# Attention's first and last probabilities scaled half by ScalarE and half by VectorE, with low parts, maxima and score products reordered

## The chip, the core and the metric

The kernel runs on one core of one Trainium2 chip. The metric is the device time of one execution in microseconds (us). Before the change three runs gave 2219.98, 2221.18 and 2222.38 us; the median is 2221.18.

The engines are named as in the profile: PE is TensorE (PEld its weight loads), DVE is VectorE, ACT is ScalarE, POOL is GpSimd, SP is the queue that issues the transfers.

## The reference

One layer of a hybrid decoder runs over 2048 prompt tokens and 64 sample tokens. The part that the change touches is sliding-window attention with 8 query heads, 2 key heads, head size 64 and a window of 128; each block of 128 queries sees its own and the previous block of keys:

```
scores = jnp.where(mask, scores, -jnp.inf)
m = jnp.maximum(jnp.max(scores, axis=-1, keepdims=True), sink)
p = jnp.exp(scores - m)
return p / (jnp.sum(p, axis=-1, keepdims=True) + jnp.exp(sink - m))
...
out = jnp.einsum('bnhgqk,bnkhd->bnqhgd', p.astype(v.dtype), vv)
```

Beside it stand the input projection, gated linear attention, the output projection and the MLP, which the change leaves as they are.

## The kernel before

**Number format.** Products are wanted at about fp32 accuracy, so nearly every operand exists twice: a rounded high part, made by ACT with a copy, and a low part, made by DVE as the source minus the high part. A product is then two or three matmuls.

**Stages.** The first stage, some 310 us, projects the tokens and does the attention; gated linear attention, the output projection and the MLP follow. The loop of this stage (lines 782 and after) runs over 16 blocks of 128 tokens, i = 0 to 15. Each iteration does the attention of block i in four **units** and in between, as filling for PE, the projection of block i + 2, the transposes of block i + 3 and the heads of block i + 1. A unit is one pair of heads: unit (i, r, jj) is key head r, pair jj; in an iteration u = 0 to 3 stand for (0,0), (0,1), (1,0), (1,1). The names in the order rows carry them: `s_11_1_0` is the score tile of block 11, r = 1, jj = 0.

**A unit's steps** (lines 457 to 527), each ended by a `yield`:

1. `sc`: four score matmuls on PE.
2. two maxima on DVE, one for each head of the pair, which also write the masked scores to `s` (the custom operation CUSTOM_DVE_ANT_0, ISA in the order rows); each gives a column of `m`.
3. two exponentials on ACT, each with its column of `m`, which also give the sums `den`.
4. reciprocal of `den` on DVE, then two multiplications of `s` by it, on DVE; in unit (1,1) both on ACT.
5. `pT`: four transposes on PE (two for each head of the pair).
6. `ph`: high part of `pT`, on ACT. 7. `pl`: low part, on DVE.
8. `av`: four matmuls of `ph` and `pl` with the values. 9. `rest`: a copy on ACT. 10. `mo`: an addition on DVE.

**What sets the order.** PE, ACT and DVE each take their instructions in the order in which the program writes them; `InOrder` (line 110) chains every call made through `te`, `ac` and `dv`. The program writes them by stepping three units through their `yield`s by hand: `now` (maxima to `ph`), `behind` (the unit before, `pl` to `mo`) and `ahead` (the unit after, `sc`). One turn of the loop over u (line 821) is called a **slot** below; slot u has unit u as `now`. POOL and SP are ordered by the scheduler.

**Other work in the slots** is placed by the table `A_PLAN` (line 58): a name, the slot, and a letter for the place within it; T stands after the first step of `now`, A after the exponentials, X after the transposes of `x`, B after `pT`, C after `ph`. What the prediction speaks of: `xT`, the transposes of block i + 3 (`x_half`, line 288), with `xh` (ACT) and `xl` (DVE); `junk`, a sum of squares on ACT in slot 2; `first` and `rest`, which scale a projection into `qk`, `glr` and `vv` on ACT, and `vl`, the low parts of `vv` and `glr` on DVE; and from `heads_T` (line 404), run in slot 2 for block i + 1, the transposes `pq` and `pk`, the high parts `qh`, `kh` and `ql` (ACT; `ql` holds the high part for r = 1 in its upper half), and the low parts `klo0`, `lo0`, `lo1` on DVE. `xT` and `pq` share one PSUM bank, so that `xT` waits until the low parts of the queries have been read from it.

**PE's filling** is `A_FILL` (line 56): so many projection matmuls at three places of each slot, 13, 12, 10 and 13 in slots 0 to 3.

Of the kernel before, what the change touches and what calls it, by code (L numbers as in the profile page):

```python
# [55 lines left out]
A_FILL = ((11, 2, 0), (10, 0, 2), (10, 0, 0), (12, 1, 0))  # L56
A_LEAD, A_SPLIT = 14, (2, 1, 0, 0)
A_PLAN = [(name, (int(at[0]), at[1])) for name, at in dict(
    klo0="3T", first="1B", hi1="3B", x1="1B", lo1="0A", x0="0C", rest="3A", lo0="3A", junk="2A", turn="1A", rstd="1A", vl="3B"
).items()]  # L60
G_FIRST = (0, 1)
G_NEXT = (NB, *range(2, NB))
# [77 lines left out]
def hybrid_step_kernel(ctx: ExitStack, tc: tile.TileContext, I, O):  # L140
# [263 lines left out]
    def heads_T(i):  # L404

        n, rot = rows(i), rots.pop(i)
        if i == NB - 1:
            stores.append((O["k_win_prompt"][0, 0].rearrange("w h d -> w (h d)"), rot[:, 4].rearrange("p r d -> p (r d)")))  # L410
        if i == NB:
            for name, new in (("k", rot[:, 4].rearrange("p r d -> p (r d)")), ("v", vals[i])):
                stores.append((new_d[name], new[:NS]))
        pq = bank([P, 4, P], "d", f"pq_{i}")
        for j in range(4):
            te.transpose(pq[:, j, :n], rot[:n, j].rearrange("p r d -> p (r d)"), ident[:n, :n])
        pk = bank([P, P], "b", f"pk_{i}")
        te.transpose(pk[:, :n], rot[:n, 4].rearrange("p r d -> p (r d)"), ident[:n, :n])
        if i == NB:
            qs = sp.tile([P, DB, 4, DT], F32, tag="tb", name="qs", bufs=1)  # L420
            ac.activation(qs, pq[:, :, :NS].rearrange("p j (b t) -> p b j t", b=DB), AF.Copy, scale=0.125)
            kns = sp.tile([P, NS], F32, name="kns")
            ac.activation(kns, pk[:, :NS], AF.Copy)
            heads[i] = qs, kns
            return {}
        qs = [sp.tile([P, 4, P], F32R, tag=t, name=f"{t}_{i}", bufs=2) for t in ("qh", "ql")]
        ks = sp.tile([P, 2, 2, P], F32R, tag="kh", name=f"kh_{i}", bufs=2)
        kl = sp.tile([P, 2, 2, P], F32R, tag="kl", name=f"kl_{i}", bufs=2)
        ac.activation(qs[0][half_of[0]], pq[half_of[0]], AF.Copy, scale=-0.125)
        for r in range(2):  # L430
            ac.activation(ks[half_of[r], r, 1, :], pk[half_of[r]], AF.Copy)
            if i > 0:
                nc.gpsimd.tensor_copy(ks[half_of[1 - r], r, 1, :], f32(ks[half_of[r], r, 1, :]))
            else:
                ac.activation(ks[half_of[1 - r], r, 1, :], pk[half_of[r]], AF.Copy)
        if i > 0:
            nc.gpsimd.tensor_copy(ks[:, :, 0, :], f32(heads[i - 1][1][:, :, 1, :]))
            nc.gpsimd.tensor_copy(kl[:, :, 0, :], f32(heads[i - 1][2][:, :, 1, :]))
        heads[i] = qs, ks, kl

        def k_lo(r):
            dv.tensor_tensor(kl[half_of[r], r, 1, :], pk[half_of[r]], f32(ks[half_of[r], r, 1, :]), op=ALU.subtract)
            nc.gpsimd.tensor_copy(kl[half_of[1 - r], r, 1, :], f32(kl[half_of[r], r, 1, :]))

        def q_lo(r):
            dv.scalar_tensor_tensor(
                qs[r][half_of[1 - r]], pq[half_of[r]], -0.125, f32(qs[r][half_of[r]]), op0=ALU.mult, op1=ALU.subtract
            )

        return {  # L450
            "klo0": lambda: k_lo(0),
            "lo0": lambda: q_lo(0),
            "hi1": lambda: ac.activation(qs[1][half_of[1]], pq[half_of[1]], AF.Copy, scale=-0.125),
            "lo1": lambda: (k_lo(1), q_lo(1)),
        }

    def unit(i, r, jj, mo):

        nkt = min(i + 1, 2)
        nk = nkt * P  # L460
        rr = half_of[r]
        u_ = f"{i}_{r}_{jj}"
        h0 = r * 4 + jj * 2
        s = sp.tile([P, 2, nk + 1], F32, tag="s", name=f"s_{u_}", bufs=3)
        nc.gpsimd.tensor_copy(s[:, :, nk : nk + 1], sink[:, h0 : h0 + 2].unsqueeze(2))
        yield
        qs, ks, kl = heads[i]
        kh, kl = (t[:, r].rearrange("p a k -> p (a k)")[:, 2 * P - nk :] for t in (ks, kl))
        sc = bank([P, 2, nk], "b", f"sc_{u_}")
        for u in range(2):  # L470
            j = jj * 2 + u
            te.matmul(sc[:, u, :], qs[r][:, j, :], kh, start=True, stop=False)
            te.matmul(sc[:, u, :], qs[r][:, j, :], kl, start=False, stop=True)
        yield
        m = sp.tile([P, 2], F32, tag="m", name=f"m_{u_}", bufs=3)
        for u in range(2):
            dv.tensor_tensor_reduce(
                s[:, u, :nk], sc[:, u, :], amask[:, 2 * P - nk :], scale=1.0,
                scalar=sink[:, h0 + u : h0 + u + 1], op0=ALU.add, op1=ALU.min, accum_out=m[:, u : u + 1],
            )  # L480
        yield
        den = sp.tile([P, 2], F32, tag="den", name=f"den_{u_}", bufs=3)
        for u in range(2):
            ac.activation(
                s[:, u, :], s[:, u, :], AF.Exp, scale=-1.0, bias=m[:, u : u + 1], accum_out=den[:, u : u + 1]
            )
        yield
        dv.reciprocal(den, den)
        for u in range(2):
            if (r, jj) == (1, 1):  # L490
                ac.activation(s[:, u, :nk], s[:, u, :nk], AF.Copy, scale=den[:, u : u + 1])
            else:
                dv.tensor_scalar(s[:, u, :nk], s[:, u, :nk], den[:, u : u + 1], None, op0=ALU.mult)
        yield
        pT = bank([P, nkt, 2, P], "c", f"pT_{u_}")
        for u in range(2):
            for kt in range(nkt):
                te.transpose(pT[:, kt, u, :], s[:, u, kt * P : (kt + 1) * P], ident)
        yield
        ph = sp.tile([P, nkt, 2 * P], F32R, tag="ph", name=f"ph_{u_}", bufs=2)  # L500
        pl = sp.tile([P, nkt, 2 * P], F32R, tag="pl", name=f"pl_{u_}", bufs=2)
        pf = pT.rearrange("p k u q -> p k (u q)")
        ac.activation(ph, pf, AF.Copy)
        yield
        dv.tensor_tensor(pl, pf, f32(ph), op=ALU.subtract)
        yield
        av = bank([P, 2 * P], "e", f"av_{u_}")
        vs = [vals[t] for t in range(i + 1 - nkt, i + 1)]
        both, hi, lo = ([v[:, r, u] for v in vs] for u in (slice(2), 0, 1))
        both = [v.rearrange("p u d -> p (u d)") for v in both]  # L510
        out = mo[rr, jj * 2 : jj * 2 + 2].rearrange("p j q -> p (j q)")
        if nkt == 1:
            te.matmul(av[:HD], hi[0], ph[:, 0], start=True, stop=False)
            te.matmul(av[:HD], hi[0], pl[:, 0], start=False, stop=False)
            te.matmul(av[:HD], lo[0], ph[:, 0], start=False, stop=True)
            yield
            ac.activation(out, av[:HD], AF.Copy)
        else:
            te.matmul(av, both[0], ph[:, 0], start=True, stop=False)
            for kt in range(2):  # L520
                te.matmul(av[:HD], hi[kt], pl[:, kt], start=False, stop=False)
            te.matmul(av, both[1], ph[:, 1], start=False, stop=True)
            yield
            rest = sp.tile([P, 2 * P], F32, tag="spc", name=f"rest_{u_}", bufs=2)
            ac.activation(rest[:HD], av[HD:], AF.Copy)
            yield
            dv.tensor_tensor(out, av[:HD], rest[:HD], op=ALU.add)
        if (r, jj) == (1, 1):
            stores.append((mix_d[i][:, 0:4, :], mo))
        yield  # L530
# [135 lines left out]
    def run(products, n=None):  # L666
        deque(products if n is None else islice(products, n), 0)
# [118 lines left out]
    for i in range(NB):  # L786
# [34 lines left out]
        for u in range(4):  # L821
            next(now)
            do(u, "T")
            next(behind, None)
            next(now)
            do(u, "A")
            later = next(queue)
            next(later)
# [2 lines left out]
            if u != 3:  # L831
                next(behind, None)
            run(fill, A_FILL[u][1])
            if u < 2 and new:
                hi, todo[f"x{u}"] = x_half(i + 3, u)
                hi()
            elif u == 2:
                todo.update(heads_T(i + 1))
            do(u, "X")
            run(fill, A_FILL[u][2])  # L840
            next(now)
            if u == 3:
                next(behind, None)
            next(behind, None)
            next(ahead)
            next(now)
            do(u, "B")
            split_some(A_SPLIT[u] if i < NB - 1 else 1)
            next(now)
            do(u, "C")  # L850
            behind, now, ahead = now, ahead, later
    for left in todo.values():
        left()
# [1263 lines left out]
```

## Time and profile before

| | |
|---|---|
| three runs | 2219.98, 2221.18, 2222.38 us |
| the profiled execution | 2222.0 us, span 2220.2 us |
| busy, whole span | PE 2172.9, DVE 1518.6, ACT 1218.7, POOL 261.7 us |
| busy, 61.58 to 284.64 us (iterations 1 to 13, from slot 2 to slot 2) | 223.06 us: PE 215.96, ACT 186.06, DVE 178.66, POOL 133.90 |

The span is the profiled execution without what lies before its first and after its last instruction. A busy time is the time in which an engine has an instruction running; PE's matmuls overlap and their ends are modelled, so that PE can look busy while it waits, and its waits are better read from the distance of the starts. In a timeline row stand start, duration, engine, line, operation, output and inputs, and in square brackets the idle time ahead of it and what ended it. Nearly all rows name line 129, that of the helper, so tiles tell them apart.

### The profile page before, as it was taken

The page shows a single profiled execution, that of the slowest core. Times are in us where ns is not written, and L with a number is a line of the kernel's source. Part 1 is how long each engine was busy: PE and PEld are TensorE (multiplying, and loading weights), DVE is VectorE, ACT ScalarE, POOL GpSimd, SP SyncE. Part 2 cuts the span into 40 slices and gives each one's busy share as a digit, 9 for nine tenths or more (in the row PEclk, how much of TensorE's full clock was granted, in tenths as well). Part 3 has the DMA queues.
Part 4 walks back from the last instruction along what each step waited for, and adds up shares of the span by engine and source line. Part 5 has one row for each costly group of instructions (what it writes and reads, how often), then busy time and mean ns, then how long its engine had stood idle before and what let it go on. Part 6 is the DMA issues. An engine that isn't in the chain of part 4 may idle for free.

```text
span 2220.2 us, 34144 instructions
## 1 busy us (share of the span) xinstructions
PE 2172.9 (98%) x11784; PEld 1863.6 (84%) x11784; DVE 1518.6 (68%) x3101; ACT 1218.7 (55%) x2626; POOL 261.7 (12%) x417
## 2 busy tenths in 40 slices
PE   8999999999999999899999999999999999999998
PEld 7889888999998888688888887888888888888886
DVE  5888777777876665788888655547776666555566
ACT  6788866556664443555555554435454545444444
POOL 3566522111111100000000000000000000000000
PEclk9999999999999999999999999999999999999999
DMA  7344322214436665867877677767553444666685
GB/s 236 121 137 146 104 90 84 67 58 132 152 110 230 205 194 192 256 218 256 277 272 244 242 238 233 235 192 259 186 186 140 148 157 147 227 199 196 194 267 188
DMA packets 240010, 411.53 MB, mean 185 GB/s; under 512 B 25877, under 2 KB 142077, under 8 KB 235725
## 3 DMA queue, kind: packets, MB, share of 16 engines
q1 hardware_dynamic: 239836, 409.35, 55.7%
q8 instruction: 93, 1.52, 0.3%
q14 instruction: 81, 0.66, 0.1%
HBM read 266.34 MB, written 143.98 MB: 185 GB/s over the span
## 4 chain that ended last, share of the span: by engine, by line
PE 77%; DVE 9%; ACT 8%; DMA 3%; issue 2%; POOL 1%; SPq 0%; DVEq 0%; ACTq 0%; POOLq 0%
PE dn L129 25%; PE gproj L129 9%; PE uc L129 7%; PE ua L129 7%; PE out L1269 6%; PE ud L129 4%; PE ub L129 4%; PE ue L129 4%; ACT s L129 2%; PE proj L129 2%; PE sam L129 1%; PE dsam L129 1%; DVE s L129 1%; PE o L129 1%; PE xT L129 1%
## 5 line engine op out<-in xcount | busy, mean ns | idle before, releaser
L129 PE MATMUL dn<-o0t,o0s 128*128 128x512 f32 x896 | 349.3, 390 | 2.4 <-ACT f L1891 1.1
L129 PE MATMUL dn<-o1t,o0s 128*128 128x512 f32 x896 | 349.5, 390 | 0.5 <-DVE o1t L217 0.5
L129 PE MATMUL dn<-o0t,o1s 128*128 128x512 f32 x896 | 349.3, 390 | 0.0
L217 DVE TENSOR_TENSOR o1s<-rs,o0s 128x512 fp32r<-128x512 f32 x224 | 154.8, 691 | 231.2 <-ACT o0s L216 228.4
L216 ACT ACTIVATE o0s<-rs 128x512 fp32r<-128x512 f32 x224 | 141.1, 631 | 305.8 <-PE dn L129 283.8
L129 PE MATMUL gproj<-wg,gx 128*128 128x384 f32 x1408 | 264.7, 342 | 2.9 <-ACT dec L1025 1.8
L129 PEld LDWEIGHTS gproj<-wg,gx 128*128 128x128 f32 x1408 | 241.0, 188 | 7.8 <-issue 3.9
L129 ACT ACTIVATE st<-st 128x512 f32<-128x512 f32 x224 | 141.2, 630 | 141.9 <-DVE st L129 137.9
L129 PEld LDWEIGHTS dn<-o0t,o0s 128*128 128x128 f32 x896 | 168.2, 188 | 39.9 <-ACT f L1891 1.5
L129 PEld LDWEIGHTS dn<-o1t,o0s 128*128 128x128 f32 x896 | 168.2, 188 | 37.4 <-DVE o1t L217 1.4
L129 PEld LDWEIGHTS dn<-o0t,o1s 128*128 128x128 f32 x896 | 168.2, 188 | 35.2
L129 PE MATMUL uc<-H,s 128*128 128x512 f32 x768 | 187.7, 393 | 1.7 <-ACT s L129 1.2
L129 PE MATMUL ua<-H,w 128*128 128x512 f32 x744 | 179.2, 390 | 0.0
L129 PEld LDWEIGHTS uc<-H,s 128*128 128x128 f32 x768 | 143.6, 189 | 33.2 <-ACT s L129 1.6
L129 PEld LDWEIGHTS ua<-H,w 128*128 128x128 f32 x744 | 139.7, 188 | 29.4
L1269 PE MATMUL out<-wo,mt 128*128 128x512 f32 x680 | 158.6, 392 | 0.0
L217 DVE TENSOR_TENSOR o1t<-rt,o0t 128x512 fp32r<-128x512 f32 x224 | 153.5, 685 | 7.5 <-ACT o0t L216 7.3
L206 POOL TENSOR_TENSOR frs<-rs_v,half 128x1 f32<-128x1 f32 (+1 forms) x13 | 10.1, 787 | 1214.7 <-DVE rs_v L204 693.5
L1269 PEld LDWEIGHTS out<-wo,mt 128*128 128x128 f32 x680 | 126.5, 188 | 26.1
L216 ACT ACTIVATE o0t<-rt 128x512 fp32r<-128x512 f32 x224 | 138.2, 617 | 8.5 <-DMA rt<-t_d 8.2
L129 DVE TENSOR_TENSOR st<-st 128x512 f32<-128x512 f32 x160 | 110.6, 691 | 26.6 <-ACT st L129 22.3
L129 ACT ACTIVATE s<-t 128x1024 fp32r<-128x1024 f32 x62 | 65.7, 1060 | 96.8 <-PE ua L129 27.9
(393 smaller groups left out, 4224.8 us busy)
## 6 DMA issues: line engine op xcount, KB each, us to landing
s_d<-st SPq DMA_DIRECT2D x32, 1792.0 KB, 9.8
rs<-s_d SPq DMA_DIRECT2D x224, 256.0 KB, 2.9
raw<-in_w_up SPq DMA_DIRECT2D x64, 512.0 KB, 4.6
rt<-t_d SPq DMA_DIRECT2D x128, 256.0 KB, 4.4
rt<-in_w_down SPq DMA_DIRECT2D x96, 256.0 KB, 3.2
t<-in_w_down SPq DMA_DIRECT2D x64, 256.0 KB, 4.1
t_d<-t SPq DMA_DIRECT2D x32, 512.0 KB, 3.4
gx<-xt_d SPq DMA_DIRECT2D x28, 512.0 KB, 6.0
```

The costliest lines, as they stand in the source:

```text
L129: ins = call(*a, **k)
L206: nc.gpsimd.tensor_tensor(out, v[:n], e, op=ALU.pow)
L216: nc.scalar.activation(hi, src, AF.Copy)
L217: vector.tensor_tensor(lo, src, f32(hi), op=ALU.subtract)
L1269: te.matmul(banks[c], x, w[:, c * 512 : (c + 1) * 512], start=k + u == 0, stop=k == KT - 1 and u == len(products) - 1,)
```

## The change

It moves five things and splits one:

- The two maxima of a unit are now two steps, and `pl` of the unit before is written between them.
- The probabilities of units (0,0) and (1,1) are scaled half by ACT (the first head) and half by DVE (the second); before, DVE did both of (0,0) and ACT both of (1,1).
- In slot 0 the score products of the next unit, the reciprocal and the scaling come ahead of the transposes `xT`; before, they came behind.
- `lo1` loses its key part, which becomes `klo1`, later in slot 0 (0B).
- `hi1`, the high part `ql`, goes behind `ph` of slot 3 (3C); `vl` goes ahead of `mo` (3S, a new letter).
- `split_some`, which splits later weights on ACT and POOL, goes behind `ph`.

```diff
-    klo0="3T", first="1B", hi1="3B", x1="1B", lo1="0A", x0="0C", rest="3A", lo0="3A", junk="2A", turn="1A", rstd="1A", vl="3B"
+    klo0="3T", first="1B", hi1="3C", x1="1B", lo1="0A", klo1="0B", x0="0C", rest="3A", lo0="3A", junk="2A", turn="1A", rstd="1A", vl="3S"
...
-            "lo1": lambda: (k_lo(1), q_lo(1)),
+            "lo1": lambda: q_lo(1),
+            "klo1": lambda: k_lo(1),
...
                 scalar=sink[:, h0 + u : h0 + u + 1], op0=ALU.add, op1=ALU.min, accum_out=m[:, u : u + 1],
             )
-        yield
+            yield
...
         for u in range(2):
-            if (r, jj) == (1, 1):
+            if u == 0 and r == jj:
                 ac.activation(s[:, u, :nk], s[:, u, :nk], AF.Copy, scale=den[:, u : u + 1])
...
             do(u, "T")
             next(behind, None)
             next(now)
+            next(now)
             do(u, "A")
...
             run(fill, A_FILL[u][1])
+            if u == 0:
+                next(ahead)
+                next(now)
             if u < 2 and new:
...
             run(fill, A_FILL[u][2])
-            next(now)
+            if u:
+                next(now)
+            do(u, "S")
             if u == 3:
                 next(behind, None)
             next(behind, None)
-            next(ahead)
+            if u:
+                next(ahead)
             next(now)
             do(u, "B")
-            split_some(A_SPLIT[u] if i < NB - 1 else 1)
             next(now)
             do(u, "C")
+            split_some(A_SPLIT[u] if i < NB - 1 else 1)
```

Three places show what it moves. The first is DVE in slot 3 of block 11, before the change: the two maxima of unit (1,1) (each with the row that writes `m`), the low part of the keys of block 12, and `pl` of unit (1,0).

```order
L129 ISA s_11_1_1_3483,m_11_1_1_3596<-sc_11_1_1_3583,amask_210,sink_413 128x256
L129 ISA m_11_1_1_3596 128x1
L129 ISA s_11_1_1_3483,m_11_1_1_3596<-sc_11_1_1_3583,amask_210,sink_413 128x256
L129 ISA m_11_1_1_3596 128x1
L129 TENSOR_TENSOR kl_12_3571<-pk_12_3566,kh_12_3570 64x128
L129 TENSOR_TENSOR pl_11_1_0_3594<-pT_11_1_0_3588,ph_11_1_0_3593 128x512
L129 SCALAR_TENSOR_TENSOR qh_12_3568<-pq_12_3561,qh_12_3568 64x512
L129 RECIPROCAL den_11_1_1_3602<-den_11_1_1_3602 128x2
```

The same place on DVE with the change:

```order
L129 ISA s_11_1_1_3483,m_11_1_1_3596<-sc_11_1_1_3583,amask_210,sink_413 128x256
L129 ISA m_11_1_1_3596 128x1
L129 TENSOR_TENSOR kl_12_3571<-pk_12_3566,kh_12_3570 64x128
L129 TENSOR_TENSOR pl_11_1_0_3594<-pT_11_1_0_3588,ph_11_1_0_3593 128x512
L129 ISA s_11_1_1_3483,m_11_1_1_3596<-sc_11_1_1_3583,amask_210,sink_413 128x256
L129 ISA m_11_1_1_3596 128x1
L129 SCALAR_TENSOR_TENSOR qh_12_3568<-pq_12_3561,qh_12_3568 64x512
L129 RECIPROCAL den_11_1_1_3602<-den_11_1_1_3602 128x2
L129 TENSOR_SCALAR s_11_1_1_3483<-s_11_1_1_3483,den_11_1_1_3602 128x256
```

The second maximum now stands behind `pl`, and `pl` reads `ph` of the unit before; half of the scaling has come to DVE.

The second place is ACT in slots 3 and 0, from `ph` of unit (1,0) on, before the change:

```order
L129 ACTIVATE ph_11_1_0_3593<-pT_11_1_0_3588 128x512
L129 ACTIVATE s_11_1_1_3483,den_11_1_1_3602<-s_11_1_1_3483,m_11_1_1_3596 128x257 x2
L129 ACTIVATE qk_13_3524<-proj_13_1_3429,rstd_all_183 128x248
L129 ACTIVATE glr_201<-proj_13_1_3429,rstd_all_183 128x2x16
L129 ACTIVATE vv_13_3607<-proj_13_1_3429,rstd_all_183 128x2x64
L129 ACTIVATE s_11_1_1_3483<-s_11_1_1_3483,den_11_1_1_3602 128x256 x2
L129 ACTIVATE rest_11_1_0_3633<-av_11_1_0_3624 64x256
L129 ACTIVATE ql_12_3569<-pq_12_3561 64x512
L129 ACTIVATE ph_11_1_1_3649<-pT_11_1_1_3641 128x512
L129 ACTIVATE s_12_0_0_3541,den_12_0_0_3668<-s_12_0_0_3541,m_12_0_0_3664 128x257 x2
```

And with it:

```order
L129 ACTIVATE ph_11_1_0_3593<-pT_11_1_0_3588 128x512
L129 ACTIVATE s_11_1_1_3483,den_11_1_1_3602<-s_11_1_1_3483,m_11_1_1_3596 128x257 x2
L129 ACTIVATE qk_13_3524<-proj_13_1_3427,rstd_all_183 128x248
L129 ACTIVATE glr_201<-proj_13_1_3427,rstd_all_183 128x2x16
L129 ACTIVATE vv_13_3607<-proj_13_1_3427,rstd_all_183 128x2x64
L129 ACTIVATE s_11_1_1_3483<-s_11_1_1_3483,den_11_1_1_3602 128x256
L129 ACTIVATE rest_11_1_0_3635<-av_11_1_0_3624 64x256
L129 ACTIVATE ph_11_1_1_3648<-pT_11_1_1_3643 128x512
L129 ACTIVATE ql_12_3569<-pq_12_3561 64x512
L129 ACTIVATE s_12_0_0_3541,den_12_0_0_3668<-s_12_0_0_3541,m_12_0_0_3664 128x257 x2
```

One multiplication is gone and `ph` stands ahead of `ql`; the two exponentials keep their place in ACT's queue.

The third place is PE at the end of slot 0, as a piece of the difference (the number behind each tile's name counts tiles and differs for that alone), in an early block:

```order
-L129 MATMUL xT_0_583<-ident,x_491 128x128 x4
-L129 MATMUL sc_0_1_592<-kh_510,qh_508 128x128
-L129 MATMUL sc_0_1_592<-kl_511,qh_508 128x128
-L129 MATMUL sc_0_1_592<-kh_510,qh_508 128x128
-L129 MATMUL sc_0_1_592<-kl_511,qh_508 128x128
+L129 MATMUL sc_0_1_581<-kh_510,qh_508 128x128
+L129 MATMUL sc_0_1_581<-kl_511,qh_508 128x128
+L129 MATMUL sc_0_1_581<-kh_510,qh_508 128x128
+L129 MATMUL sc_0_1_581<-kl_511,qh_508 128x128
+L129 MATMUL xT_0_591<-ident,x_491 128x128 x4
```

The four transposes have moved behind the four score products; in every other respect PE's order is what it was.

## The prediction

> **What bounds the kernel now.** The sum is made against the profiled execution, 2222.0 us with a span of 2220.2 us; the median of the three runs, 2221.18, lies 0.8 us below it. A measurement of this kernel can tell some 0.2% from no change, 4.4 us. The first view is busy time by window, since the change touches only the attention loop: one iteration, from slot 2 to the next slot 2, with its length, then busy time (and instructions) of PE, PEld, DVE, ACT and POOL, the granted clock and DMA.
>
> ```profile
> 234.07:251.11 17.04, 16.62 (x112) 15.29 (x111) 13.76 (x43) 14.02 (x39) 8.29 (x16) 1.00 0.25 93
> ```
>
> PE looks full, but ACT and DVE are at four fifths, so a chain that alternates between engines can set the pace. The second view is the chain that ended last, over this iteration (start, duration, engine, tile):
>
> ```profile
> 234.77 0.60 ACT ph L129
> 235.37 0.98 ACT s L129 x4
> 236.35 0.62 ACT junk L129
> ...
> 237.41 0.38 ACT rest L129
> 237.82 0.59 ACT qh L129
> ...
> 238.89 0.60 ACT ph L129
> 239.49 0.98 ACT s L129 x4
> 240.47 0.35 ACT qk L129
> 240.82 0.18 ACT glr L129
> 241.00 0.26 ACT vv L129
> 241.26 0.81 ACT s L129 x2
> 242.09 0.39 ACT rest L129
> 242.50 0.42 DVE mo L129
> ...
> 244.24 0.60 DVE pl L129
> 244.87 0.29 DVE kl L129
> 245.20 0.70 DVE ql L129
> 245.95 0.67 PE xT L129 x4
> ```
>
> From 234.77 to 242.09, slots 2 and 3, the chain never leaves ACT: `ph`, both exponentials, `junk`, `rest`, `qh`, `kh`, the next `ph`, both exponentials, `qk`, `glr`, `vv`, the scaling. There ACT works without a gap and sets the pace. In slot 0 the chain goes over DVE (`pl`, `kl`, `ql`) to the transposes `xT`. So the change must be judged by what it puts into ACT's queue in slots 2 and 3, and by what it takes from DVE's in slot 0.
>
> **Slots 2 and 3: the split maxima.** The rows that price it, DVE first:
>
> ```profile
> 234.10 0.69 DVE L129 TENSOR_TENSOR xl<-xT,xh 128x512 fp32r<-128x512 f32 x1 [0.21 <-ACT xh L129]
> 234.71 0.47 DVE L129 CUSTOM_DVE_ANT_0 s<-sc,amask,sink 128x256 f32<-128x256 f32 x1
> ...
> 239.52 0.69 DVE L129 TENSOR_TENSOR pl<-pT,ph 128x512 fp32r<-128x512 f32 x1 [0.27 <-ACT ph L129]
> ...
> 243.35 0.48 DVE L129 CUSTOM_DVE_ANT_0 s<-sc,amask,sink 128x256 f32<-128x256 f32 x1
> ```
>
> and ACT:
>
> ```profile
> 235.76 0.50 ACT L129 ACTIVATE s<-s,m 128x257 f32<-128x257 f32 x1
> ...
> 239.88 0.50 ACT L129 ACTIVATE s<-s,m 128x257 f32<-128x257 f32 x1
> ...
> 241.16 0.91 ACT L129 ACTIVATE s<-s,den 128x256 f32<-128x256 f32 x2
> ...
> 243.93 0.51 ACT L129 ACTIVATE s<-s,m 128x257 f32<-128x257 f32 x1 [0.21 <-DVE m L129]
> ```
>
> Three offsets follow. `pl` starts 0.63 us after the start of its `ph` (238.89 to 239.52; DVE had waited for it). A low part keeps the next DVE instruction 0.61 back (234.10 to 234.71). An exponential starts 0.58 after the start of its maximum (243.35 to 243.93, where ACT had waited for `m`).
>
> Before, both maxima ran while ACT was still at `ph`, and the exponentials followed it without a gap. Now the second maximum stands behind `pl`, and `pl` waits for `ph`. The second exponential therefore comes 0.63 + 0.61 + 0.58 = 1.82 after the start of `ph`, whatever the rest does. In slot 2: 234.77 + 1.82 = 236.59 where it was at 235.76, **0.83 later**. It is at the head of ACT's queue; `junk`, `rest`, `qh`, `kh` and the next `ph` stand behind it back to back and come 0.83 later too, `ph` at 239.72. In slot 3 the same again: 239.72 + 1.82 = 241.54 instead of 239.88, 1.66 later.
>
> Behind it in slot 3 come `qk`, `glr`, `vv` and now one multiplication in place of two. The first one started 1.28 after the exponential (239.88 to 241.16) and took half of 0.91: it ends at 241.54 + 1.28 + 0.46 = 243.28. DVE's half is ready before that, since it needs only `den`. What PE does with it is in these rows:
>
> ```profile
> 234.43 0.42 PE L129 MATMUL proj<-wa_hi,xh 128*128 128x392 f32 x1
> ...
> 241.72 0.84 PE L129 MATMUL pT<-ident,s 128*128 128x128 f32 x4
> 242.31 0.42 PE L129 MATMUL proj<-wa_hi,xl 128*128 128x392 f32 x1
> ...
> 244.35 0.28 PE L129 MATMUL av<-ph,vv 128*128 128x256 f32 x1
> 244.90 0.45 PE L129 MATMUL av<-pl,vv 128*64 128x256 f32 x2 [0.27 <-DVE pl L129]
> 245.18 0.28 PE L129 MATMUL av<-ph,vv 128*128 128x256 f32 x1
> 245.30 0.34 PE L129 MATMUL proj<-wa_lo,xh 128*128 128x392 f32 x1
> 245.48 0.34 PE L129 MATMUL proj<-wa_hi,xl 128*128 128x392 f32 x1
> 245.95 0.66 PE L129 MATMUL xT<-ident,x 128*128 128x128 f32 x4
> ...
> 247.27 0.42 PE L129 MATMUL proj<-wa_hi,xh 128*128 128x392 f32 x1
> ...
> 251.11 0.60 PE L129 MATMUL pT<-ident,s 128*128 128x128 f32 x4
> 251.46 0.43 PE L129 MATMUL proj<-wa_hi,xh 128*128 128x392 f32 x1
> ```
>
> `pT` of unit (1,1) followed its first half after 0.10 (241.16 + 0.46 = 241.62, 241.72) and then took until 242.31, since the second half came late; four transposes without a wait take 0.35 (251.11 to 251.46). New: 243.28 + 0.10 + 0.35 = 243.73 instead of 242.31. **Slots 2 and 3 lose 1.42 us.** Of the 1.66, the half taken from ACT gives back a quarter. The two `av` and the score products of these slots wait too, inside this time.
>
> [...] The row at 234.71 starts before the one ahead of it has ended, so the trace decides for 0.61.
>
> **Slot 0: what goes.** `av` of unit (1,1) waited for `pl`: 0.55 between 244.35 and 244.90, of which such a matmul takes 0.12 (245.18 to 245.30); 0.43 goes, because `ph` no longer stands behind `ql`, and `pl` no longer behind the second maximum. `xT` waited for `ql`: 245.95 instead of 245.48 + 0.18 = 245.66 (a projection takes 0.18, 245.30 to 245.48); 0.29 goes, because the key part is gone ahead of `ql` and the score products stand ahead of `xT`. Together **0.72**. What is late next: the second exponential of (0,0). `ql` now fills ACT between `ph` and the exponentials, so its gap there is only some 0.3. The scaling of (0,0) in two halves ends before PE is through the score products and `xT`.
>
> **Slot 1: what comes.** `xh` waits for `xT`, which is later; `xl`, the first maximum, `pl` and the second maximum follow it on DVE in one line, and the half multiplication that ACT took on lies ahead of `xh`. By the same offsets `av` of (0,0) and then `pT` of (0,1) come 0.3 later relative to the slot than now. Bounds: 0 (PE's ten projections cover it) and 0.65, if DVE also carries the delay into slot 2, where the first maximum must not be later than `ph`. I take **0.30**.
>
> **Moved, at nothing.** `klo1` has until the score products of slot 1, over 3 us away. `vl` is read by the next block's `av`. `split_some` behind `ph` lies in the gap of slot 1. `ql` behind `ph` is counted above. POOL's copies wait for the same tiles, and POOL is idle half the time; the SP queue keeps its transfers. If this cover went, POOL's copies of `kl` would cost some 0.3 an iteration.
>
> **The sum** for an iteration: 1.42 − 0.72 + 0.30 = **+1.00 us**. Full iterations run from i = 1 to 13; these two rows are the transposes ahead of slot 2 in blocks 1 and 14:
>
> ```profile
> 61.58 0.60 PE L129 MATMUL pT<-ident,s 128*128 128x128 f32 x4
> ...
> 284.64 0.60 PE L129 MATMUL pT<-ident,s 128*128 128x128 f32 x4
> ```
>
> 13 iterations give +13. Block 0 has half the keys, and blocks 14 and 15 have neither `xT` nor `junk`, so that ACT has room for its gaps; I take them together at +0.5 (0 to +1.5). 2222.0 + 13.5 = 2235.5 by the profiled execution, 2234.7 by the median: **2234.5**. Lower end: half of slot 3's own 0.83 is hidden, 1.00 − 0.42 = +0.58 an iteration, 2229. Upper end: DVE's lag is carried on (1.42 − 0.72 + 0.65 = +1.35), 2239.
>
> **The rivals.**
>
> *Faster*: the gaps in ACT cost nothing, because PE has work of its own meanwhile, and what is left is slot 0: 13 × 0.72 = 9.4 less, 2212. It decides the other way from the point where ACT has over 1.4 us of room in slots 2 and 3. For it speaks that ACT is idle 3.0 us in 17.04; against, that the chain shows it at work from 234.77 to 242.09. Chance 0.14.
>
> *No change*: the two cancel, because only one of the two delays reaches PE (0.83 − 0.72 = 0.11 an iteration, 1.4 in all; the other would have to be hidden by the projections of slot 3): 2223, and with the bound of a measurement 2217 to 2226. Against it: `pT` of (1,1) follows ACT's scaling by 0.10, so nothing hides there. Chance 0.11.
>
> *Still slower*: each of the four units, not two, leaves ACT its 0.83 idle, and DVE lags into slot 2: +1.7 an iteration, 2243. In slots 0 and 1 `ql` and DVE's own waits lie in that place, so 0.05.
>
> *The change doesn't do what it says*: the order of the instructions shows every move; left out.
>
> **How the numbers follow.** Forecast (slower by 7 to 18 us, 2229 to 2239) 0.70; rivals as above. Slower by over 0.2%: 0.70 + 0.05 = 0.75; within 0.2%: 0.11; faster: 0.14. The range takes in the forecast and the case without a change, 0.81: 2217 to 2240. The forecast's own range is 2229 to 2239.
>
> **What would show it.** In ACT's rows of slots 2 and 3 the second exponential has some 0.8 idle ahead of it with `m` as its releaser, where now there is none; the iteration is 18.0 instead of 17.04; `pT` of (1,1) waits on `s` by over a microsecond; the waits of `av` for `pl` and of `xT` for `ql` in slot 0 are gone. The prediction is wrong if ACT shows these gaps and the distance of the iterations doesn't grow, or if the second exponential doesn't wait.

## The result and the profile after

The changed kernel took 2237.19 us (median of six runs, 2236.04 to 2242.54) beside 2222.84 us before (six runs, 2219.98 to 2224.82): the ratio is 1.0071, with a 95% interval of 1.0061 to 1.0080. It is 14.35 us slower. The profiled execution of the changed kernel took 2239.22 us, 2.0 above its own median; the sums below are between the two profiled executions, 17.2 us apart.

First the iteration, the same stretch of the program as in the prediction (from `pT` of unit (11,0,1) to that of (12,0,1)), as one row and then slot by slot, 2, 3, 0, 1. The columns are length, then busy time and instructions of PE, PEld, DVE, ACT and POOL, the granted clock, DMA share, GB/s:

```profile
242.16:259.85 17.69, 16.60 (x111) 15.40 (x110) 14.30 (x44) 14.28 (x39) 8.21 (x16) 1.00 0.25 90
```

```profile
242.16:245.97 3.81, 3.81 (x29) 3.69 (x28) 3.10 (x11) 3.25 (x8) 0.19 (x1) 1.00 0.69 275
245.97:251.37 5.40, 4.41 (x27) 3.63 (x25) 3.85 (x13) 4.61 (x16) 2.19 (x6) 1.00 0.19 49
251.37:255.56 4.19, 4.19 (x29) 4.19 (x30) 3.81 (x11) 3.44 (x9) 4.03 (x6) 1.00 0.02 4
255.56:259.85 4.29, 4.20 (x30) 3.88 (x29) 3.54 (x12) 2.97 (x8) 1.79 (x6) 1.00 0.15 61
```

The iteration grew from 17.04 to 17.69 us, +0.65, with the busy times of PE and ACT nearly what they were: the time is waiting, and it lies in slot 3. ACT's rows show where:

```profile
242.87 0.60 ACT L129 ACTIVATE ph<-pT 128x512 fp32r<-128x512 f32 x1
243.63 0.51 ACT L129 ACTIVATE s<-s,m 128x257 f32<-128x257 f32 x1 [0.16 <-DVE m L129]
...
244.63 0.51 ACT L129 ACTIVATE s<-s,m 128x257 f32<-128x257 f32 x1 [0.40 <-DVE m L129]
...
247.78 0.60 ACT L129 ACTIVATE ph<-pT 128x512 fp32r<-128x512 f32 x1
...
249.53 0.51 ACT L129 ACTIVATE s<-s,m 128x257 f32<-128x257 f32 x1 [0.67 <-DVE m L129]
```

The second exponential starts 1.76 and 1.75 us after the start of its `ph`, with `m` as its releaser, where before no exponential of these slots had idle time ahead of it. The chain that ended last, in the same stretch, now leaves ACT for DVE at the place that the prediction named:

```profile
247.78 0.61 ACT ph L129
...
248.41 0.69 DVE pl L129
249.10 0.39 DVE s L129
249.49 0.02 DVE m L129
...
249.53 0.60 ACT s L129 x2
```

Over the 13 iterations from 61.47 to 294.61 us, the waits of ACT for `m` came to 53, with 22.6 us (in sum, times, the longest). The 13 iterations together grew by only 10.1 us, so not all of this wait reaches the time:

```profile
ACT s L129 <- DVE m L129: 22.6, 53, 0.7
```

Then the marks along the stage. These are PE's transposes `pT` of units (1,0,1), (14,0,1) and (15,1,1) in the changed kernel:

```profile
61.47 0.67 PE L129 MATMUL pT<-ident,s 128*128 128x128 f32 x4
...
294.61 0.57 PE L129 MATMUL pT<-ident,s 128*128 128x128 f32 x3
...
323.26 0.66 PE L129 MATMUL pT<-ident,s 128*128 128x128 f32 x4 [0.60 <-ACT s L129]
```

and the last of them before:

```profile
308.11 0.75 PE L129 MATMUL pT<-ident,s 128*128 128x128 f32 x4
```

| stretch | before | after | difference |
|---|---|---|---|
| start to (1,0,1) | 61.58 | 61.47 | -0.1 |
| 13 iterations, (1,0,1) to (14,0,1) | 223.06 | 233.14 | +10.1 |
| (14,0,1) to (15,1,1), the last blocks | 23.47 | 28.65 | **+5.2** |
| the rest of the program | | | +2.0 |

Eleven of the 13 iterations grew by 0.63 on average, and the two around block 4 (from (3,0,1) to (5,0,1)) by 3.2 together, 1.9 more than two such. The second row is less than the +13 of the forecast, the third was forecast at next to nothing. In the third there is a second cause, and it shows around block 4 too: the splitting of the later weights (`split_some`), which the change put behind `ph`. ACT makes the rounded high part of a weight, called a cast below, and DVE or POOL the low part, all named `wg`. In block 15 ACT splits one piece in every slot. ACT, then DVE, in slot 0 of block 15:

```profile
307.99 0.60 ACT L129 ACTIVATE ph<-pT 128x512 fp32r<-128x512 f32 x1 [0.75 <-PE pT L129]
308.49 0.61 ACT L129 ACTIVATE wg<-wg_raw,gcol 128x384 fp32r<-128x384 f32 x1
310.37 0.51 ACT L129 ACTIVATE s<-s,m 128x257 f32<-128x257 f32 x1 [1.27 <-DVE m L129]
```

```profile
309.13 0.62 DVE L129 SCALAR_TENSOR_TENSOR wg<-wg_raw,gcol,wg 128x384 fp32r<-128x384 f32 x1 [1.43 <-ACT wg L129]
309.78 0.48 DVE L129 CUSTOM_DVE_ANT_0 s<-sc,amask,sink 128x256 f32<-128x256 f32 x1
```

DVE's low part `wg` stands ahead of the next unit's maxima in DVE's queue, and waits 1.43 us for ACT's high part, which now comes only after `ph`; so the first maximum and its exponential are late. Before, in the same slot, ACT made the high part in its gap ahead of `ph`, and DVE didn't wait:

```profile
295.72 0.60 ACT L129 ACTIVATE wg<-wg_raw,gcol 128x384 fp32r<-128x384 f32 x1
297.25 0.60 ACT L129 ACTIVATE ph<-pT 128x512 fp32r<-128x512 f32 x1 [0.92 <-PE pT L129]
```

```profile
297.14 0.62 DVE L129 SCALAR_TENSOR_TENSOR wg<-wg_raw,gcol,wg 128x384 fp32r<-128x384 f32 x1
297.68 0.48 DVE L129 CUSTOM_DVE_ANT_0 s<-sc,amask,sink 128x256 f32<-128x256 f32 x1
```

### The profile page after: what moved, and what is told of

It is laid out like the page before. It is cut to its first block, busy times and chain, and to the rows that moved or that the text cites. A ratio compares the mean times of both kernels' runs of the same rounds, so it can differ in the third digit from the quotient of the medians.

```text
span 2237.1 us, 34112 instructions
## 1 busy us (share of the span) xinstructions
PE 2174.4 (97%) x11784; PEld 1868.4 (84%) x11784; DVE 1526.4 (68%) x3101; ACT 1223.4 (55%) x2626; POOL 260.4 (12%) x417
## 4 chain that ended last, share of the span: by engine, by line
PE 80%; DVE 8%; ACT 7%; DMA 3%; issue 2%; POOL 1%; SPq 0%; DVEq 0%; ACTq 0%; POOLq 0%
PE dn L129 26%; PE gproj L129 10%; PE uc L129 7%; PE ua L129 7%; PE out L1277 6%; PE ue L129 4%; PE ud L129 4%; PE ub L129 4%; PE proj L129 3%; ACT s L129 2%; DVE s L129 2%; PE sam L129 1%; PE dsam L129 1%; PE o L129 1%; DVE pl L129 1%
## 5 line engine op out<-in xcount | busy, mean ns | idle before, releaser
L206 POOL TENSOR_TENSOR frs<-rs_v,half 128x1 f32<-128x1 f32 (+1 forms) x13 | 10.1, 785 | 1215.5 <-DVE rs_v L204 695.6
## 6 DMA issues: line engine op xcount, KB each, us to landing
s_d<-st SPq DMA_DIRECT2D x32, 1792.0 KB, 10.1
```

Source lines behind the costliest of these rows:

```text
L206: nc.gpsimd.tensor_tensor(out, v[:n], e, op=ALU.pow)
```

## The experiments

Twelve kernels, each timed in five rounds against the kernel before. "Iteration" is a stretch from slot 2 to slot 2, as above, 17.04 us before and 17.69 after; its one row has the columns shown above.

**The theory**: the loss is the wait of the second exponential for a maximum behind `pl`, in slots 2 and 3, where ACT has no room. **The rivals**: the moved score products and halves cost, or the moved weights do.

### E1: both maxima in one step again

The changed kernel, with one edit:

```diff
-            yield
+        yield
+        yield
```

> The changed kernel with both maxima of a unit together again, ahead of the low part of the unit before; all else as changed. Theory (the second maximum behind the low part leaves ACT idle in slots 2 and 3): the idle time ahead of the second exponentials is gone there, slot 3 falls from 5.4 us to some 4.0 and the iteration from 17.7 to some 16.4, so 13 iterations give back 17 us: 2219 to 2222, no slower than the kernel before. Rival (the halves and the new order in slot 0 cost it): the iteration stays at 17.7 and the time at 2237.

Measured: 2221.83 us, ratio 0.9998 (0.9989 to 1.0007), 15.4 us less than the changed kernel.

```profile
232.58:249.21 16.63, 16.15 (x112) 15.42 (x111) 14.48 (x44) 13.92 (x39) 8.26 (x16) 1.00 0.25 96
```

The iteration is 16.63, 1.06 less than with the split and 0.41 less than before: 13 × 1.06 = 13.8 of the 15.4. So in the loop the split carries the loss, and the rest of the change gains. Yet the time is that of before: blocks 14 and 15 took 27.33 us, 3.9 more than before, with the weights still behind `ph`.

### E2: the split alone

The kernel before, with the maxima split and `pl` between them:

```diff
-        yield
+            yield
...
             next(now)
+            next(now)
             do(u, "A")
```

> The kernel before with the two maxima split around the low part and nothing else. Theory: slots 2 and 3 lose 1.66 us an iteration (no half is taken from ACT's scaling here) and slot 0 keeps its wait of the transposes for the low part of the queries, so the iteration is 18.7 or more: 2244 to 2252, slower than the changed kernel. Rival: 2223, as before.

Measured: 2245.33 us, ratio 1.0103 (1.0089 to 1.0117).

```profile
212.89:231.49 18.60, 17.05 (x111) 15.23 (x110) 13.79 (x44) 15.17 (x41) 11.74 (x20) 1.00 0.35 124
```

The iteration is 1.56 longer than the same one before (slots 2, 3, 0, 1: 3.87, 5.41, 5.21, 4.11). It is one with two casts; the iteration that is shown for the kernel before, which has none, took 18.35 here, 1.31 longer and under the 18.7 that was expected. Nothing but the split was touched, and alone it costs more than beside the rest of the change (1.06).

### E3 and E8: the split in two of the four slots

The changed kernel, where only units with r = 0 (E3) or r = 1 (E8) have the step between their maxima. The edit of E3:

```diff
-            yield
+            if r == 0 or u == 1:
+                yield
+        if r == 1:
+            yield
```

> The changed kernel with the maxima split only in slots 0 and 1 and together in slots 2 and 3. Theory: ACT has no idle time in slots 2 and 3, and slots 0 and 1 keep what the split gives them (the low part earlier): iteration some 16.1, 2214 to 2218, faster than the kernel before and a little faster than with the maxima together everywhere. Rival: 2237 as changed.

> The changed kernel with the maxima split only in slots 2 and 3. Theory: the loss stays whole, since it lies there, and slot 1 also has its wait of av for pl back (4.67 against 4.3): iteration some 18.1, 2238 to 2244, no faster than the changed kernel. Rival (the split costs in slots 0 and 1, where ACT took on a half): 2224 to 2230.

Measured: E3 2222.0 us, 0.9999 (0.9990 to 1.0007); E8 2241.19 us, 1.0083 (1.0069 to 1.0097). The iterations, E3 and then E8:

```profile
216.30:232.85 16.55, 16.47 (x111) 15.39 (x110) 14.32 (x44) 14.21 (x39) 8.21 (x16) 1.00 0.39 137
```

```profile
209.72:227.72 18.00, 16.51 (x112) 15.44 (x110) 14.67 (x44) 14.82 (x41) 11.77 (x20) 1.00 0.37 128
```

The place is settled: against E1 a split with r = 1 costs 1.4 us an iteration, one with r = 0 next to nothing; beside each other they cost less (17.69), as the second shortens slot 1. E3's time was a miss. Its iteration is only 0.08 better than E1's: slot 1 gains 0.37, but slots 2 and 3 lose 0.23 and 0.12, where DVE comes out of slot 1 without a pause and its first maximum of slot 2 is late (ACT waits 0.16 for it). And the stretches around block 4 and in blocks 14 and 15 keep their loss.

### E4, E11, E5: the weights back ahead of `ph`

E4 is the changed kernel with `split_some` at its old place in block 15 only; E11 has it there in all blocks. The edit of E11:

```diff
             do(u, "B")
+            split_some(A_SPLIT[u] if i < NB - 1 else 1)
             next(now)
             do(u, "C")
-            split_some(A_SPLIT[u] if i < NB - 1 else 1)
```

E5 is E1 with the same edit: all of the change but the split and the moved weights.

> The changed kernel with the splitting of later weights put back ahead of the high part in block 15 alone. There the trace shows the first maximum of each slot waiting on DVE behind the low part of a weight, which waits for ACT's high part, which waits behind ph. Theory: this costs some 3 of the 14 us; 2233 to 2235. Rival (block 15 loses by the split maxima like the others): 2236 to 2238.

> The changed kernel with one edit: the splitting of the later weights back at its old place ahead of ph in all blocks; the maxima stay split. Theory with two additive causes: the weights cost 5.35 us beside maxima together, so 2237.2 - 5.4 = 2231.8 us (2230 to 2233); the iteration stays near 17.7 us, and blocks 4, 14 and 15 get short again. Rival, that the two causes overlap (the gap that the split maximum leaves in ACT's queue is the very place that the casts fill): the gain is 0 to 3 us, 2234 to 2237.

> The changed kernel with the maxima together and with the splitting of later weights back ahead of the high part everywhere; the halves, the order in slot 0 and the moved parts stay. Theory (what the change loses is the split maxima, and the moved weights in blocks 4 and 15): blocks 4 and 15 give back 1.4 and 3.4 us against the kernel with the maxima together alone, the iteration stays at 16.6: 2216 to 2219, faster than the kernel before. Rival (the moved weights cost nothing): 2222, as with the maxima together alone.

Measured: E4 2235.26 us, 1.0059 (1.0046 to 1.0073); E11 2235.92 us, 1.0062 (1.0048 to 1.0075); E5 **2216.48 us, 0.9977 (0.9966 to 0.9987)**, faster than before. The last blocks of E4:

```profile
295.10:320.38 25.28, 23.39 (x154) 21.11 (x154) 19.59 (x60) 19.39 (x54) 7.15 (x13) 1.00 0.27 82
```

They give back 3.4 of the 5.2 us, in E11 as well. In the time E4 shows 1.9 us of that, and its interval overlaps that of the changed kernel, so this rests on the traces. Beside maxima together (E5 against E1) the edit is worth 5.35 us by the medians; in the traces blocks 14 and 15 give back 4.0 (27.33 to 23.37), and the iterations around block 4 nothing, where 1.4 had been expected. In the changed kernel the edit is worth only 1.3, so my additive theory falls. Two iterations of E11 show why, the first with two casts `wg` on ACT and the second with none:

```profile
209.22:227.24 18.02, 16.66 (x112) 15.42 (x110) 14.38 (x44) 15.02 (x41) 11.70 (x20) 1.00 0.38 128
227.24:244.94 17.70, 16.60 (x112) 15.39 (x110) 14.26 (x44) 14.30 (x39) 8.19 (x16) 1.00 0.34 122
```

Ahead of `ph` the casts cost 0.32 in each such iteration (about seven, 2.2 us); behind it they lie in the gap that the split leaves in ACT's queue. Two losses of the change share one place, and taking one away uncovers the other.

### E6 and E7: halves alone, order alone

E6 is the kernel before with `if u == 0 and r == jj:` in the scaling; E7 is before with slot 0 in the new order, `klo1`, `hi1` and `vl` moved, and nothing else.

> The kernel before with the two halves and nothing else. Theory: the transposes of unit (1,1) no longer wait 0.24 us for ACT's second half, and ACT's half of (0,0) lies in a gap: iteration 16.8, 13 times 0.24, 2218 to 2220. Rival (the halves are part of the loss, since ACT's half of (0,0) stands ahead of the high part): 2223 to 2227.

> The kernel before with the order of slot 0 (score products ahead of the transposes), the key part moved, ql behind ph and vl ahead of mo; no halves, no split maxima, weights where they were. Theory: slot 0 loses its two waits and slot 1 takes some back, as with the maxima together: iteration 16.8 to 16.9, 2218 to 2221. Rival (the order of slot 0 costs): 2223 to 2227.

Measured: E6 2222.24 us, 0.9994 (0.9985 to 1.0003); E7 2223.06 us, 1.0002 (0.9993 to 1.0011). Neither time can be told from that of before, and both forecasts, some 1 to 4 us faster, were missed. Their iterations are 17.15 and 16.87, where both together (E5) give 16.64. In E6 ACT's half of unit (0,0) stands behind `xh`, and PE's `pT` waits 0.61 us for it; in the new order it stands ahead. So by the iterations the halves pay only with the order.

### E9, E10, E12: what ends last in the better version

E9 is E5 with `x0="1A"`, so that in slot 1 `xl` stands behind `pl`.

> The version with both maxima together and the moved weights back ahead of ph, with one more edit: in slot 1 VectorE makes the rounded low part xl of the next block's normed rows behind pl instead of ahead of it. Theory that VectorE's order in slot 1 still sets its length: av of unit (0,0) no longer waits about 0.5 us for pl behind xl, slot 1 goes from 4.67 to about 4.2 us, the iteration from 16.64 to about 16.2, times 13 about -5.5 us: 2210 to 2213 us. Rival, that VectorE only hands xl's 0.61 us on to the reciprocal, the scaling and so pT of unit (0,1): iteration and time as without the edit, 2216 to 2217 us, with the wait moved from av to pT or proj.

Measured: 2215.19 us, 0.9969 (0.9957 to 0.9981), between the two forecasts. Against E5 that isn't settled by the time, the intervals overlap; the trace has two kinds of iteration, the first with casts `wg`, the second without:

```profile
198.60:215.43 16.83, 16.36 (x111) 15.42 (x110) 14.41 (x43) 14.61 (x41) 11.84 (x20) 1.00 0.40 139
215.43:231.55 16.12, 16.11 (x112) 15.44 (x111) 14.31 (x44) 13.84 (x39) 8.28 (x16) 1.00 0.36 130
```

Without casts slot 1 is 4.15, as the theory had it; with them it is 4.87, longer than E5's 4.67. ACT's queue shows the reason, and DVE's answer:

```profile
211.25 0.93 ACT L129 ACTIVATE wg<-wg_raw 128x384 fp32r<-128x384 f32 x2
212.08 0.59 ACT L129 ACTIVATE ph<-pT 128x512 fp32r<-128x512 f32 x1
```

```profile
212.70 0.69 DVE L129 TENSOR_TENSOR pl<-pT,ph 128x512 fp32r<-128x512 f32 x1 [0.61 <-ACT ph L129]
```

The casts hold `ph` back, DVE stands idle ahead of `pl`, and `xl` no longer fills that time. E10 therefore moves them behind the exponentials of slot 1:

```diff
             do(u, "A")
+            if u == 1 and i < NB - 1:
+                split_some(3)
...
-            split_some(A_SPLIT[u] if i < NB - 1 else 1)
+            split_some(0 if i < NB - 1 else 1)
```

> The version with both maxima together and xl behind pl, with the splitting of the later weights (two casts wg on ACT, 0.93 us, in seven blocks) moved from the place ahead of ph of slot 0 to the place behind the exponentials in slot 1. Theory that ACT's queue ahead of ph sets slot 1 in those blocks: the idle 0.61 us of VectorE ahead of pl goes, slot 1 falls from 4.88 to about 4.15 to 4.3 us as in the blocks without casts, seven times 0.6 to 0.7 us: about 2211 us. Rival, that the casts behind the exponentials push rest and xh of slot 1 back by as much as they release ph: 2215 us, slot 1 or slot 2 longer by what the other gains.

Measured: 2215.1 us, 0.9964 (0.9951 to 0.9976), though most iterations with casts fell to some 16.4. Block 4 gained nothing: its wait for POOL only moved, from slot 1 (4.16 us, where E9 has 7.44) into slot 2, whose columns alone these are:

```profile
108.83:117.69 8.86, 5.65 (x29) 4.87 (x28) 3.77 (x11) 6.31 (x16) 5.31 (x7) 0.82 0.47 141
```

8.86 us instead of 3.87: ACT waited 3.58 us for POOL, whose multiplications of the first weights by their gains stood behind work that waited for DVE and PE; `rest`, `xh` and `ph` stood behind the waiting cast, PE stood still for 2.38 us, and then its granted clock was 0.62 and 0.52 by stretches of 2 us from 114 to 118. E12 splits the first weights of block 4 in slot 3:

```diff
-            if u == 1 and i < NB - 1:
+            if u == (3 if i == 4 else 1) and i < NB - 1:
```

> The version with the casts wg behind the exponentials of slot 1, where in block 4 TensorE stood still for about 2.4 us and slot 2 took 8.86 us, at a granted clock of 0.62 and 0.52 for 4 us behind the pause. One edit: block 4 splits its weights in slot 3 instead of slot 1, when GpSimd has multiplied them. Theory that the pause is ACT's cast waiting for GpSimd, and that the lower clock follows from the pause: without it slot 2 of block 4 goes to about 3.9 us, slot 3 grows by the 0.93 us of the casts, and the granted clock between 110 and 120 us stays at 1.00: 4 us less, 2211 us. Rival, that the clock falls there whatever PE does: the pause goes and the lower clock stays, 2 us less, 2213 us. Second rival, GpSimd's multiplications stand as late for block 5: 2215 us.

Measured: **2211.0 us, 0.9945 (0.9931 to 0.9958)**, the lowest of all, with an interval that still touches those of E9 and E10. The same slot, by the same columns:

```profile
109.63:113.33 3.70, 3.70 (x29) 3.70 (x28) 2.88 (x9) 3.46 (x10) 1.75 (x3) 1.00 0.35 142
```

The pause is gone, and the clock stayed at 1.00 there, as the theory had it. That such a pause always brings the lower clock is not shown: the last section has one of 3.07 us, in E4, with the clock at 1.00.

## Why the prediction was right, and where it wasn't

**Slots 2 and 3, the split maxima: right in size, and in mechanism for slot 3.** `ph` to second exponential was 1.75 us (predicted 1.82). In slots 2 and 3, counted as in the prediction to the first projection behind `pT` of (1,1), the loss was 1.38 us (1.42):

```profile
251.78 0.43 PE L129 MATMUL proj<-wa_hi,xl 128*128 128x392 f32 x1
```

251.78 − 242.16 = 9.62, where before it was 242.31 − 234.07 = 8.24. E1, E2 and E8 show the cause. Two things differ from the prediction's account. In slot 2 `pl` did not wait for `ph`: it started at 243.52 (in DVE's rows below) without idle time ahead of it, at the end of a row of DVE work, just after `ph` had ended at 243.47. DVE's lag out of slot 1, which the prediction had in its upper bound alone, gave the same time there, by coincidence. And `pT` of (1,1) was to wait on `s` for over a microsecond; PE's idle time there was 0.30, since PE had already waited before it, most of all at the score products:

```profile
250.36 0.36 PE L129 MATMUL sc<-kh,qh 128*128 128x256 f32 x1 [0.46 <-DVE qh L129]
...
251.37 0.66 PE L129 MATMUL pT<-ident,s 128*128 128x128 f32 x4 [0.30 <-ACT s L129]
```

**The offset of 0.61 between a low part and what follows on DVE: right.** These rows of the changed kernel have it as 249.02 − 248.41 = 0.61: the maximum starts before the 0.69 that `pl` lasts are over.

```profile
243.52 0.68 DVE L129 TENSOR_TENSOR pl<-pT,ph 128x512 fp32r<-128x512 f32 x1
...
248.41 0.69 DVE L129 TENSOR_TENSOR pl<-pT,ph 128x512 fp32r<-128x512 f32 x1 [0.34 <-ACT ph L129]
249.02 0.47 DVE L129 CUSTOM_DVE_ANT_0 s<-sc,amask,sink 128x256 f32<-128x256 f32 x1
```

**Slot 0: right, a little too small.** From that projection to the next `pT` it took 255.56 − 251.78 = 3.78 where it had been 246.91 − 242.31 = 4.60: a gain of 0.82 (0.72). The waits of `xT` for `ql` and of `av` for `pl` are gone.

**Slot 1: too large.** 4.29 after 4.20, +0.09, where I took 0.30. The lower bound, PE's projections as cover, was nearer. E3 shows DVE's lag going into slots 2 and 3 (0.23 and 0.12); in the changed kernel it falls together there with the wait of the split maxima.

**The sum for an iteration: too large for that.** 1.38 − 0.82 + 0.09 = 0.65, not 1.00; over 13 iterations 8.2 to 8.5 us instead of 13.

**"`split_some` behind `ph` lies in the gap of slot 1", and blocks 0, 14 and 15 at +0.5 (0 to +1.5): wrong.** This is the step that failed. For the iterations in between it holds, and better than said (E11). But it took that place for all, and two others cost. Blocks 14 and 15 lost 5.2 us, of which E4 shows 3.4 to be the moved weights: DVE's low part `wg` waits for ACT, ahead of the maxima. The other 1.8 are the split, where I had expected room in ACT's queue: E11 and E5 differ in it alone, and took 25.28 and 23.37 us there. The two iterations around block 4 cost another 1.9: ACT's first cast, which had waited 1.40 us for POOL, now waits 3.16 with the exponentials behind it, and POOL has `rstd_all`, which waits for DVE, ahead of the multiplications of these weights. ACT, then POOL, with the change:

```profile
114.74 0.52 ACT L129 ACTIVATE wg<-wg_raw 128x384 fp32r<-128x384 f32 x1 [3.16 <-POOL wg_raw L259]
...
115.95 0.49 ACT L129 ACTIVATE s<-s,m 128x257 f32<-128x257 f32 x1
```

```profile
113.36 0.56 POOL L206 TENSOR_TENSOR rstd_all<-rs_v,half 128x1 f32<-128x1 f32 x1 [1.34 <-DVE rs_v L129]
113.88 1.61 POOL L259 TENSOR_TENSOR wg_raw<-wg_raw,gcol 128x384 f32<-128x384 f32 x2
```

POOL's order went with the place of the weights: `rstd_all` stands first in each of the five kernels that have `split_some` behind `ph` (the changed one, E1, E3, E4, E8), where this wait is 3.16 to 3.17 us, and second in each that has it ahead (before, E2, E5, E6, E7, E9, E11), where it is 1.40 to 1.89. The old place doesn't always shorten the block, though: slot 1 of block 4 was 7.8 us in E11 and 8.0 in E5, and 7.5 in the changed kernel. In both PE paused for about 2 us there (2.00 and 1.87), and its granted clock over the 10 us from 110 to 120 was 0.83 in each, where it was 1.00 before.

So that the total came out near the forecast is in part luck: 13 iterations at 0.35 too much (4.6 us) and, at 6.6 us too little, block 4 and the last blocks nearly cancel. The remaining 2.0 us of the profiled execution lie behind the stage, 1.6 of them at a lower clock, 0.50 at its lowest (last section); the median has less.

**The rivals.** "Faster" failed at its condition, as the gap reaches PE. But its reasoning on slot 0 is what E5 shows: without the split, and with the weights back, the new order and the halves gain 6 us. "Still slower" had each of the four units pay for the split; by E3 those of slots 0 and 1 don't.

## What to carry to other kernels

Before an instruction is put between two that another engine waits for, look at which engine its own input comes from: here the two maxima ran ahead of ACT, and one `pl` between them tied DVE back to ACT, for 1.06 us an iteration. Price a moved step at each place where it runs, above all at its first and last runs, where its input is latest or its low part stands on another engine's queue. And where a gain doesn't show in the time, look for a stretch that has lost: E10's shorter iterations stood beside a slot of 8.86 us, and with that mended E12 is 4.1 us faster by the medians.

## What the runs showed of the hardware

In some runs a pause of PE cost more than its length, in others it didn't. In block 4 of the changed kernel PE waited 3.06 us; these are the rows around it, and the granted clock (third column from the right) by stretches of 2 us:

```profile
117.76 0.68 PE L129 MATMUL pT<-ident,s 128*128 128x128 f32 x4 [3.06 <-DVE s L129]
...
119.69 0.53 PE L129 MATMUL proj<-wa_hi,xl 128*128 128x392 f32 x1
120.02 0.53 PE L129 MATMUL proj<-wa_hi,xh 128*128 128x392 f32 x1
```

```profile
118.00:120.00 2.00, 2.00 (x10) 2.00 (x9) 2.00 (x6) 1.67 (x5) 1.01 (x2) 0.63 0.77 233
120.00:122.00 2.00, 2.00 (x9) 2.00 (x9) 0.99 (x5) 1.64 (x4) 0.83 (x1) 0.52 1.03 416
```

From 118.71 to 121.00 us the projections came 0.33 apart, and from 123.71 on 0.18. E4 has the same pause at the same place, and there the clock stayed at 1.00 and the projections, from 119.39 on, 0.18 apart:

```profile
118.69 0.67 PE L129 MATMUL pT<-ident,s 128*128 128x128 f32 x4 [3.07 <-DVE s L129]
```

```profile
118.00:120.00 2.00, 1.31 (x9) 1.28 (x10) 1.97 (x6) 1.97 (x4) 0.66 (x3) 1.00 0.55 140
```

With that the two iterations around block 4 were 0.45 us shorter in E4. Nor does the length decide among the other runs: at this place the clock fell behind pauses of 1.87 us (E5) and 2.00 (E11), to 0.83 over the 10 us from 110 to 120, and behind 2.38 (E10), to 0.62 and 0.52 as above. Behind 1.20 (before) it stayed at 1.00, and behind 2.12 (E7) and 2.64 us (E1) the projections came 0.18 apart.

Between the two first transposes of the gated linear attention (343.3 and 371.0 us before, 358.1 and 387.4 after) the changed kernel lost 1.6 us to a lower clock, 0.88, 0.50 and 0.77 by stretches of 2 us from 373 to 379, behind a wait of 1.81. The kernel before has that wait as well (1.82), with the clock at 1.00. In block 4 seven of the 14 profiled executions show the lower clock (the changed kernel, E3, E5 and E8 to E11), and what decides it no run here settles.
